# Sliding-window attention: unscaled sums joined by row transfers, and background steps queued behind projections

## The chip, the cores and the metric

The kernel runs on one core of a Trainium2 chip. The metric is the device time of one execution in microseconds (us). Before the change it was 1960.81 us, the median of three runs (1959.38, 1973.70 and 1960.81).

## What is computed

The reference is one inference step of a two-layer decoder with 1024 channels, for a prompt of 1024 tokens and 8 further requests ("samples") with one new token each, 1032 columns in all. Each layer is

```python
h = rms_norm(x);  y = concat(branch(h) * silu(gate(h))) @ w_out;  x = x + rms_norm(y)
```

The even layer has three branches of four heads of 128: a gated delta net (GDN), a dilated sliding-window attention and a cross attention to a memory of 256 rows. The odd layer has a gated linear recurrence (RG-LRU) and the memory attention. Local attention has, for each head, three groups with dilation 1, 4 and 16, each with a query, key and value projection of its own and a window of its own. Each prompt query takes a softmax per group, and the three are merged by their denominators. With m the largest score of a group, l the sum of exp(score - m) and num the sum of exp(score - m) v, a query's result is

```python
M = max(m0, m1, m2);  f_g = exp(m_g - M)
out = sum_g(f_g * num_g) / sum_g(f_g * l_g) * silu(gate)
```

In group 1 the tokens lie ordered by their remainder modulo 4, in group 2 modulo 16, so a query has another place in each group's tiles. The samples' queries attend to caches in HBM (2048 positions at dilation 1, 4, 16, and the memory): "cached attention".

## The kernel before, in words

Channels lie on the 128 partitions, tokens along the free axis. The columns are cut into chunks of 352, 336 and 344. A projection (`proj`, L166) loads 128 output channels of weights (SyncE issues the DMA, 512 KB), splits them in a high and a low part (ScalarE copies, L152; GpSimd or VectorE subtracts, L154), and runs for each chunk 8 x 3 matmuls into one PSUM bank (`mm3`, L162 to L164), so 72 per projection. ScalarE drains the bank (L440, L443). Projections take four rotating banks ("p") in this stage, other work on TensorE takes three ("a") and cached attention one ("c").

The stages are: inputs and norms; `even_gdn` (GDN with its convolutions, chains per head, and the memory heads 0 to 3 between them, to about 650 us); `even_swa` (L902, local attention, about 600 to 1240 us); `out_layer(0)` (L1290); `odd`; `out_layer(1)`. A scheduler of the language orders the instructions on each engine by the kernel's text and priorities, and each engine works through its list in order.

In `even_swa` each of four heads h goes through three groups g. For each there are three projections (q, k, v, tiles `sw`; weights `ws` h g c) and then scores `ss` (TensorE L979), mask and row maximum `P`, `sm` (VectorE L981), and exp with the row sum `sl` (ScalarE L988). Five of the projections of head 0 and its gate are computed earlier, inside `even_gdn` (`swa_ahead`), and reloaded. When the three groups of a head are done, maxima and sums of groups 1 and 2 are brought into the token order of group 0: eight DMAs write them to a DRAM scratch `sd` one element at a time (L995, L999), one reads it back as `al` (L1001). Small VectorE operations of 128x8 and one exp make the scales (`mall`, `sf`, L1005 to L1016), which go out to `fd` (L1017) and come back in group order in four DMAs as `fl` (L1020, L1024). Then the probabilities `P` are scaled in place (VectorE L1055), transposed (`st`, TensorE L1058), copied to SBUF (`spt`, ScalarE L1062) and multiplied by v (`so`, L1064), and the groups are added in `sacc` (VectorE L1072). The result is multiplied by the gate (L917) and written to `mixd`, the DRAM buffer in which the heads of all branches meet. Head 3's gate (weights `wb3`) and, for two other heads, theirs are projected at the end of the stage.

`cached` (L341) does one head of cached attention for the samples: the query row goes to DRAM (`qmd`, `sqd`) and comes back on 16 partitions each (`mqb`, `sqb`), keys and values come from the cache, GpSimd multiplies (L348, L369), VectorE reduces (L349, L370), TensorE joins partitions (`mx`, `po`). Memory heads are named `mc` layer head, local heads `sc` head. Memory heads 0 to 3 and local heads 0 to 2 stand in `even_swa`, local head 3 in `out_layer(0)`.

`out_layer` (L1290) takes the mixed heads as 12 tiles, in the order of the list `order`: it loads each as `mf` (L1284) and splits it into `mah` (L1279, ScalarE) and `mal` (L1280, VectorE), multiplies eight times by a weight tile (`wo` layer m) for the first two chunks, and then eight times for the third chunk from tiles `mbh`, `mbl`, which also hold the samples' columns. The post-norm (`po`) follows chunk by chunk.

Bulk copies of the caches to the outputs (`o_sw1s` to `o_sw3s`, about 1 MB each) are issued by SyncE, one behind each weight load (L151); the prompt's new keys and values (`o_sw1p` to `o_sw3p`) are issued by ScalarE.

## Time and profile before

| | |
|---|---|
| median of three runs | 1960.81 us |
| span of the profiled execution | 1979.3 us |
| TensorE busy | 1788.5 us (90%) |
| VectorE, ScalarE, GpSimd busy | 1086.6, 705.0, 544.1 us |
| share of the chain that ended last | TensorE 65%, VectorE 14%, DMA 13% |

The profiled execution is a run of its own: its span runs from the first to the last instruction of the trace, it is 0.9% longer than the median, and no device time is listed for it apart from the span. Durations and gaps below are from it. "Granted clock" is the TensorE clock as a share of the full 2.4 GHz; its other level is 1.2 GHz, at which matmuls take about twice as long and count as busy. So time is lost both where TensorE is idle and where it is busy at the low clock.

### The profile page before, as it was taken

How to read it: one execution, taken by the hardware profiler on the slowest of the kernel's cores; microseconds unless marked ns; L12 is line 12 of the kernel's file. 1: busy time of each engine (PE TensorE's matmuls, PEld its weight loads, DVE VectorE, ACT ScalarE, POOL GpSimd, SP SyncE). 2: the span in 40 equal slices, each digit the busy share in tenths (PEclk: the TensorE clock that was granted, in tenths of full speed). 3: DMA queues.
4: the chain of work that ended last, by engine and by line, in shares of the span. 5: the costliest groups of instructions: out<-in, count | busy, mean ns of one | idle time of the engine just before them, and what ended most of it. 6: DMA issues, size and time to landing. Idle time of an engine off the chain costs nothing.

```text
span 1979.3 us, 29251 instructions
## 1 busy us (share of the span) xinstructions
PE 1788.5 (90%) x11337; PEld 1727.8 (87%) x11337; DVE 1086.6 (55%) x2391; ACT 705.0 (36%) x1590; POOL 544.1 (27%) x367
## 2 busy tenths in 40 slices
PE   6999998898998977978987987999799999999996
PEld 6899987898998877978987986899699999898996
DVE  7787759436653232224323427648854766747545
ACT  5355533122332322422422323334533434426432
POOL 3422214222111131133133203312643434330201
PEclk9999998998998988998998997999899999999998
DMA  8435464633335664466676454536572533213454
GB/s 282 174 136 205 150 200 168 208 113 134 135 123 183 152 150 118 119 158 149 142 150 151 119 101 124 166 120 226 202 244 101 181 108 117 77 49 119 141 185 141
DMA packets 206411, 297.83 MB, mean 150 GB/s; under 512 B 73312, under 2 KB 168128, under 8 KB 204352
## 3 DMA queue, kind: packets, MB, share of 16 engines
q1 hardware_dynamic: 106640, 208.09, 34.7%
q10 hardware_dynamic: 99632, 87.88, 14.8%
q8 instruction: 89, 1.46, 0.3%
q14 instruction: 50, 0.41, 0.1%
HBM read 246.54 MB, written 137.37 MB: 194 GB/s over the span
## 4 chain that ended last, share of the span: by engine, by line
PE 65%; DVE 14%; DMA 13%; ACT 4%; issue 2%; ACTq 1%; SPq 1%; POOL 0%; DVEq 0%; POOLq 0%
DMA fd<-sf 3%; DMA sd<-sl 2%; DMA al<-sd 2%; PE ss L979 1%; PE so L1064 1%; DVE tm L677 1%; PE ms L316 1%; PE mo L337 1%; DMA fl<-fd 1%; DMA mc00v<-cache_mem 1%; PE gz L800 1%; PE gt L805 1%; DVE P L1055 1%; DMA mf<-mixd 1%; DVE lacc L1216 1%
## 5 line engine op out<-in xcount | busy, mean ns | idle before, releaser
L981 DVE CUSTOM_DVE_ANT_0 P<-ss,cs 128x128 f32<-128x128 f32 (+1 forms) x96 | 33.0, 351 | 83.4 <-PE ss L979 83.0
L1064 PE MATMUL so<-spt,svt 128*128 128x128 f32 x280 | 43.3, 301 | 16.0 <-ACT spt L1062 13.1
L571 DVE SCALAR_TENSOR_TENSOR acc<-pre,vec,acc 128x1024 f32<-128x1024 f32 x36 | 49.3, 1368 | 13.4 <-ACT acc L569 13.2
L1369 POOL TENSOR_TENSOR y<-y,xr 128x352 f32<-128x352 f32 (+2 forms) x24 | 23.0, 960 | 121.6 <-DVE y L1368 104.1
L988 ACT ACTIVATE P<-P,snm 128x128 f32<-128x128 f32 (+1 forms) x96 | 42.4, 443 | 38.6 <-DVE snm L983 37.5
L1064 PEld LDWEIGHTS so<-spt,svt 128*128 128x128 f32 x280 | 40.4, 214 | 17.4 <-ACT spt L1062 17.4
L1055 DVE TENSOR_SCALAR P<-P,fl 128x128 f32<-128x128 f32 (+1 forms) x64 | 21.5, 414 | 56.4 <-DMA fl<-fd 56.4
L1062 ACT COPY spt<-st 128x384 f32<-128x384 f32 (+2 forms) x48 | 22.2, 477 | 82.1 <-PE st L1058 29.0
L1314 DVE TENSOR_TENSOR ya<-ya,ysq 128x352 f32<-128x352 f32 (+2 forms) x42 | 25.6, 610 | 40.0 <-ACT ysq L1313 39.9
L979 PE MATMUL ss<-sw,sw 128*128 128x128 f32 (+1 forms) x192 | 45.1, 323 | 0.6 <-DVE sm L981 0.6
L322 ACT ACTIVATE pm<-ms,nm 128x256 f32<-128x256 f32 x64 | 29.7, 471 | 42.5 <-DVE nm L320 26.5
L1058 PE MATMUL st<-cs,P 128*128 128x128 f32 x140 | 26.1, 303 | 16.3 <-DVE P L1055 16.3
L337 PE MATMUL mo<-mpt,vt 128*128 128x512 f32 x64 | 33.2, 600 | 4.8 <-DVE gnr L120 3.2
L336 DVE COPY mpt<-mt 128x512 f32<-128x512 f32 x32 | 22.0, 688 | 27.0 <-PE mt L334 26.9
L1171 DVE TENSOR_SCALAR lacc<-lpre,vec 128x1024 f32<-128x1024 f32 x8 | 21.4, 2673 | 25.6 <-ACT lpre L1166 25.6
L1058 PEld LDWEIGHTS st<-cs,P 128*128 128x128 f32 x140 | 19.9, 159 | 17.2 <-issue 8.7
L316 PE MATMUL ms<-kt,qm 128*128 128x256 f32 x128 | 33.7, 388 | 0.0
L979 PEld LDWEIGHTS ss<-sw,sw 128*128 128x128 f32 x192 | 32.0, 189 | 1.2 <-DVE sm L981 0.9
L1328 POOL COPY mg<-mixs 128x8 f32<-128x8 f32 x24 | 8.9, 370 | 86.2 <-DVE mbl L1331 12.5
L1174 DVE SCALAR_TENSOR_TENSOR lacc<-lpre,vec,lacc 128x1024 f32<-128x1024 f32 x24 | 32.3, 1346 | 0.2
L677 DVE TENSOR_TENSOR tm<-bl,xi 128x1 f32<-128x1 f32 (+30 forms) x31 | 30.3, 977 | 2.6 <-DMA bl<-aqd 2.1
L318 DVE TENSOR_REDUCE nm<-ms 128x2 f32<-128x512 f32 x32 | 22.0, 686 | 17.6 <-PE ms L316 17.6
(2142 smaller groups left out, 7293.6 us busy)
## 6 DMA issues: line engine op xcount, KB each, us to landing
o_sw3s<-cache_swa SPq DMA_DIRECT2D x64, 1023.5 KB
o_sw2s<-cache_swa SPq DMA_DIRECT2D x16, 1022.0 KB
gaq<-aqd ACTq DMA_DIRECT2D x20, 512.0 KB
mf<-mixd SPq DMA_DIRECT2D x20, 344.0 KB
aqd<-aq ACTq DMA_DIRECT2D x4, 1024.0 KB
o_sw3p<-sw ACTq DMA_DIRECT2D x8, 512.0 KB
mixd<-lgt ACTq DMA_DIRECT2D x8, 512.0 KB
o_sw1s<-cache_swa SPq DMA_DIRECT2D x8, 508.0 KB
```

What stands on the lines that cost most here:

```text
L316: T.matmul(ps[:, b * 256:(b + 1) * 256], q[:, (b0 + b) * P:(b0 + b + 1) * P], kt[:, h, :], start=True, stop=True)
L322: S.activation(pr[:, b2 * 2 + b, :], ps[:, b * 256:(b + 1) * 256], AF.Exp, bias=nm[:, b0 + b:b0 + b + 1], scale=SC, accum_out=lt[:, b0 + b ...
L337: T.matmul(po, vt[:, kb, h, :], st, start=kb == 0, stop=kb == 1)
L571: V.scalar_tensor_tensor(acc, pre[:, j:j + 1024], vc("gconv", ti * 4 + j), acc, ALU.mult, ALU.add)
L677: V.tensor_tensor(t3, bl[:, 0:i, i][:, None, :].broadcast_to([P, i, i]), xi[:, 0:i, 0:i].rearrange("p j c -> p c j"), ALU.mult)
L979: T.matmul(po, q[:, bb * P:(bb + 1) * P], k[:, k0:k0 + w], start=True, stop=True)
L981: V.tensor_tensor_reduce(dst, po, mask, 1.0, NEG, ALU.add, ALU.max, accum_out=m[:, g, bb:bb + 1])
L988: S.activation(dst, dst, AF.Exp, bias=nm[:, g, bb:bb + 1], scale=SC, accum_out=l[:, g, bb:bb + 1])
L1055: V.tensor_scalar(dst, dst, fs, None, op0=ALU.mult)
L1058: T.transpose(tr[:, w:w + P], dst[:, j * P:(j + 1) * P], ident)
L1064: T.matmul(po[:, (bb % 4) * P:(bb % 4 + 1) * P], vtk[g][:, kb, :], pt[:, o:o + P], start=st, stop=sp_)
L1174: V.scalar_tensor_tensor(acc[:, :1024], pre[:, j:j + 1024], vc("lconv", ti * 4 + j), acc[:, :1024], ALU.mult, ALU.add)
```

## The change

The diff below is cut to its core.

- **Background steps.** `start` puts a generator in one of the lanes "cached", "group" and "combine". `tick`, called behind each chunk of a projection (and each chunk of `out_layer`), takes one step from each lane and pins its instructions behind the last instruction issued so far on every engine. `drain_lanes` runs what is left.
- **Groups.** Each group's scores, exp, transposes and products (`group`) run in six such steps, behind the chunks of the projections that follow. The probabilities stay unscaled; the sums `num` (tiles `snum`, three) are copied out of PSUM by ScalarE, in group order.
- **Join.** `combine` transposes maxima and sums of a head into 48 rows (`slt`, `srow`), writes them to `sd` as rows of 512 bytes, reads them as 8 rows by seven DMAs (`al`, token order of each group), makes the scales on 8x128 tiles, writes `fd`, reads each group's 1024 scales back on all partitions (`sfb`, 512 KB each), and multiplies and adds the three `num` on VectorE. The joins of heads 0 to 2 run behind the next head's chunks, that of head 3 is drained at the end of the stage.
- **Moves.** Gates of local heads 1 to 3 and query and gate of memory head 3 are projected in `even_gdn`, kept in DRAM and reloaded. The memory attention of head 3 (`mem_attend`) moves from there to the end of `even_swa`. Cached attention becomes steps of the lane "cached": in `even_swa` memory heads 0 to 2 and local heads 0 to 2, in `out_layer(0)` local head 3 and memory head 3, drained behind the eighth weight tile. `o_sw1p` to `o_sw3p` are issued by SyncE. In `order`, memory head 3 and local head 3 (11 and 7) are last. The cached attention of the odd layer becomes steps too.

```diff
+    def tick():
+        for lane in list(lanes):
...
+            last = {}
+            for i in reversed(nc.cur_bb.bb.instructions):
+                if i.engine in pinned and i.engine not in last:
+                    last[i.engine] = i
...
+            with ExitStack() as after:
+                for ins in last.values():
+                    after.enter_context(tc.issue_after(ins))
+                try:
+                    j[1] = next(j[0]) - 1
...
-                if h < 3:
+                if h < 2:
                     mem_head(h + 1)
                 else:
-                    for key in ((0, 0, 1), (0, 0, 2),):
+                    for key in ((), (), (("q3",), ("g3",), (1,)), ((0, 0, 1), (0, 0, 2), (2,), (3,)))[h]:
                         swa_ahead(me, x, key)
...
+            def combine(h, ml, nums, done):
+                ps = ptile(f"slt{h}")
+                T.transpose(ps[0:48, :P], ml.rearrange("p i g b -> p (i g b)"), ident)
+                rows = sp.tile([48, P], F32, name=f"srow{h}", tag="srow", bufs=1)
+                S.copy(rows, ps[0:48, :P])
...
+                nc.sync.dma_start(out=sd.rearrange("i g b p -> (i g b) p"), in_=rows)
+                yield 1
...
+                nc.sync.dma_start(out=al[:, :, 0, :], in_=sd[:, 0].rearrange("i b p -> b i p"))
...
+                for i in range(2):
+                    for nb in range(2):
+                        nc.sync.dma_start(out=al[nb * 4:nb * 4 + 4, i, 1, :].rearrange("a (r n) -> a r n", r=4),
+                                          in_=s1[nb][:, i])
+                    nc.sync.dma_start(out=al[:, i, 2, :].rearrange("b (q n) -> b q n", q=16), in_=s2[i])
+                yield 2
...
+                S.activation(f, f, AF.Exp, scale=SC)
...
+                nc.sync.dma_start(out=fd.rearrange("g (b p) -> b g p", b=8), in_=f)
+                yield 1
...
+                    fb = sp.tile([P, 1024], F32, name=f"sfb{h}{g}", tag="sfb", bufs=2)
+                    nc.sync.dma_start(out=fb, in_=fd[g][None, :].broadcast_to([P, 1024]))
...
+                V.tensor_tensor(nums[0], nums[0], gt, ALU.mult)
+                done(nums[0])
...
+                    start("group", group(h, g, raw, ml, nums))
+                    if g == 2 and h < 3:
+                        lanes["group"].append([then("combine", combine(h, ml, nums, lambda acc, h=h: put(h, acc))), 0])
                 for f, i in (((mem_cached, 0), (mem_cached, 1)), ((mem_cached, 2), (swa_cached, 0)),
-                             ((mem_cached, 3), (swa_cached, 1)), ())[h]:
-                    f(ca, 0, i)
+                             ((swa_cached, 1), (swa_cached, 2)), ())[h]:
+                    start("cached", f(ca, 0, i))
+            sh0.close()
+            xa = mix_tiles(0, sxa)
...
+            drain_lanes("cached", "group", "combine")
+            mem_attend(sp, 0, 3, qm, gm, gm, tags=("spr", "spt"))
+            mix_put(xa, order[-2], gm)
...
+            start("combine", combine(3, ml, nums, lambda acc: last.update(acc=acc)))
             w0 = out_weights(0, 0, "a")
-            for k in order[:-1]:
+            for k in order[:-2]:
                 mix_load(0, xa, k)
+                tick()
+            drain_lanes("combine")
+            mix_put(xa, order[-1], last["acc"])
...
+            for f in late:
+                start("cached", f(ca))
             for m in range(8):
                 one(m, (0, 1), xs, "a", None if m else w0)
-                if late:
-                    late.pop(0)(ca)
+                if m == 7:
+                    drain_lanes("cached")
...
-    order = [0, 1, 2, 3, 8, 9, 10, 11, 4, 5, 6, 7]
+    order = [0, 1, 2, 3, 8, 9, 10, 4, 5, 6, 11, 7]
...
-    late = [lambda ca: swa_cached(ca, 0, 3)]
+    late = [lambda ca: swa_cached(ca, 0, 3), lambda ca: mem_cached(ca, 0, 3)]
```

Three places show how the instructions are moved (lines of the kernel before in the first list of each pair, of the changed one in the second; the number behind a name tells tiles of one name apart).

The first is VectorE at the join of head 0, which before stands in one piece (`mc01` is cached attention of memory head 1):

```order
L1013 TENSOR_TENSOR mall_6662<-mall_6662 128x8
L1014 TENSOR_TENSOR mall_6662<-mall_6662 128x8
L357 TENSOR_REDUCE mc01mr<-mc01mx 1x8
L1015 RECIPROCAL mall_6662<-mall_6662 128x8
L359 COPY mc01mr<-mc01mr 1x8x16
L1016 SCALAR_TENSOR_TENSOR sf_6663<-sf_6663,mall_6662 128x24
L361 COPY mc01mq<-mc01mr 1x128
L1055 TENSOR_SCALAR P_6145<-P_6145,sf_6663 128x128
```

```order
L996 TENSOR_SCALAR snm_7342<-sml_6903 128x2
L421 TENSOR_REDUCE mc00op<-mc00v_7210 128x128
L1052 TENSOR_TENSOR smm_7390<-al_7284 8x128
L1053 TENSOR_TENSOR smm_7390<-smm_7390,al_7284 8x128
L498 COPY sqkv<-ws110p_7407 128x8
L994 ISA spr_7341,sml_6903<-ss_7434,cs 128x256
L994 ISA sml_6903 128x1
L1054 TENSOR_TENSOR sf_7391<-al_7284,smm_7390 8x128
```

Afterwards the join of head 0 (`al`, `smm`, `sf`) stands among the score steps of head 1 (L994, L996), and no scaling of probabilities follows it.

The second is TensorE at the end of `even_swa`, where the first matmuls of `out_layer(0)` (`wo00p`) follow:

```order
L1058 MATMUL st_10861<-cs,P_9377 128x128 x2
L1064 MATMUL so_10831<-spt_10846,svt_10260 128x128 x2
L355 MATMUL sc2mx<-cs,sc2sm 1x128
L1064 MATMUL so_10851<-spt_10857,svt_10260 128x128 x2
L1064 MATMUL so_10851<-spt_10866,svt_10260 128x128 x2
L362 MATMUL sc2mx<-cs,sc2mq 128x1
L162 MATMUL wo00p_10956<-mah_10704,wo00ah_10874 128x352
L163 MATMUL wo00p_10956<-mal_10705,wo00ah_10874 128x352
```

```order
L352 MATMUL ms_10727<-kt_278,smq_10583 128x256 x2
L370 MATMUL mt_10740<-cs,pm_10719 128x128 x4
L373 MATMUL mo_10739<-mpt_10745,vt_279 128x512
L370 MATMUL mt_10748<-cs,pm_10719 128x128 x4
L373 MATMUL mo_10739<-mpt_10753,vt_279 128x512
L1032 MATMUL slt_10778<-cs,sml_9307 48x128
L162 MATMUL wo00p_10887<-mah_10581,wo00ah_10768 128x352
L162 MATMUL wo00p_10939<-mah_10581,wo00ah_10768 128x336
L162 MATMUL wo01p_11010<-mah_10581,wo01ah_11005 128x352
L162 MATMUL wo01p_11051<-mah_10581,wo01ah_11005 128x336
```

Afterwards ten of the twelve tiles of `wo00` and `wo01` (both chunks, all four "p" banks) stand before `mem_attend`'s last half; behind the transpose `slt` of the join of head 3 come only the 24 matmuls for the last two tiles, 11 and 7.

The third is TensorE in `out_layer(0)`. Before, the last step of memory head 3 stands in the midst of the projections of local head 3; afterwards the whole second half of it stands behind the first matmuls of the third chunk (`wo00p` to `wo02p`, from `mbh`, `mbl`):

```order
L163 MATMUL ws302p_9589<-h0l_115,ws302h_9557 128x336
L373 MATMUL mc03po<-cs,mc03op 128x8
L164 MATMUL ws302p_9589<-h0h_114,ws302l_9558 128x336
L162 MATMUL ws302p_9589<-h0h_116,ws302h_9557 128x336
L163 MATMUL ws302p_9589<-h0l_117,ws302h_9557 128x336
```

```order
L162 MATMUL wo02p_12266<-mbh_11326,wo02bh_12255 128x344
L163 MATMUL wo02p_12266<-mbl_11327,wo02bh_12255 128x344
L164 MATMUL wo02p_12266<-mbh_11326,wo02bl_12256 128x344
L405 MATMUL mc03mx<-cs,mc03sm 1x128
L414 MATMUL mc03my<-cs,mc03mq 128x1
L426 MATMUL mc03po<-cs,mc03op 128x8
L185 MATMUL po00c<-cs,ya_10925 128x1 x3
L426 MATMUL mc03po<-cs,mc03op 128x8
L427 MATMUL mc03po<-cs,mc03sm 128x8
L162 MATMUL wo00p_11937<-mbh_11822,wo00bh_11932 128x344
```

Between the query's transpose `mq03t`, which stands behind the last matmul of `wo07` for the first two chunks, and `mc03mx` there are 72 matmuls.

## Rows read from the trace of the kernel before

**Rows 1.** The page: span, and busy time of TensorE (matmuls).
```profile
span 1979.3 us, 29251 instructions
...
PE 1788.5 (90%) x11337; PEld 1727.8 (87%) x11337; DVE 1086.6 (55%) x2391; ACT 705.0 (36%) x1590; POOL 544.1 (27%) x367
```

**Rows 2.** Stretches: start:end, length, busy PE, PEld, DVE, ACT, POOL, granted clock, DMA share.
```profile
600.00:660.00 60.00, 48.65 (x280) 46.62 (x279) 19.56 (x67) 13.62 (x35) 11.92 (x5) 0.89 0.59 203
720.00:770.00 50.00, 26.84 (x156) 26.17 (x155) 12.39 (x47) 7.75 (x16) 8.53 (x4) 0.76 0.60 138
880.00:920.00 40.00, 22.93 (x129) 22.28 (x128) 10.97 (x42) 5.93 (x13) 5.43 (x3) 0.74 0.62 108
1030.00:1070.00 40.00, 19.01 (x107) 18.35 (x107) 9.62 (x41) 4.55 (x10) 1.35 (x2) 0.74 0.65 113
1170.00:1260.00 90.00, 65.81 (x387) 62.59 (x386) 53.51 (x82) 25.41 (x51) 20.76 (x16) 0.85 0.41 111
```

**Rows 3.** The chain that ended last, 712 to 766 us: start, us, what.
```profile
713.00 0.63 SPq L999
...
714.35 8.32 DMA sd<-sl
722.75 12.39 DMA al<-sd
...
737.39 13.36 DMA fd<-sf
...
751.47 7.36 DMA fl<-fd
...
765.82 0.29 PE ws110p L164
```

**Rows 4.** Waits 560 to 1260 us: who for whom, us in total, times, longest.
```profile
DVE P L1055 <- DMA fl<-fd: 56.4, 4, 15.6
DVE mall L1005 <- DMA al<-sd: 54.6, 4, 16.0
...
ACT ws022h L152 <- DMA o_sw1p<-sw: 25.3, 1, 25.3
...
ACT spt L1062 <- DMA o_sw2s<-sr1r: 13.1, 1, 13.1
```

**Rows 5.** Groups of instructions on the page: busy and mean ns, idle before, releaser.
```profile
L981 DVE CUSTOM_DVE_ANT_0 P<-ss,cs 128x128 f32<-128x128 f32 (+1 forms) x96 | 33.0, 351 | 83.4 <-PE ss L979 83.0
...
L322 ACT ACTIVATE pm<-ms,nm 128x256 f32<-128x256 f32 x64 | 29.7, 471 | 42.5 <-DVE nm L320 26.5
...
L336 DVE COPY mpt<-mt 128x512 f32<-128x512 f32 x32 | 22.0, 688 | 27.0 <-PE mt L334 26.9
```

**Rows 6.** Tiles `mf` and `mqb`: instructions, duration ns min/median/max, first and last start.
```profile
L1280 DVE TENSOR_TENSOR mal<-mf,mah x20: 851/869/2780, 1216.7 to 1821.6; 128x688 fp32r<-128x688 f32 x20
...
L348 POOL TENSOR_TENSOR mc03k<-mc03k,mqb x2: 2386/2396/2406, 1010.7 to 1013.0; 128x1024 f32<-128x1024 f32 x2
```

**Rows 7.** Groups of instructions on VectorE, 560 to 1260 us, shapes apart.
```profile
L370 DVE TENSOR_REDUCE sc2op<-sc2v 128x128 f32<-128x1152 f32 x3 | 6.7, 2218 | 0.0
...
L917 DVE TENSOR_TENSOR sacc<-sacc,sg 128x1024 f32<-128x1024 f32 x3 | 5.1, 1710 | 0.0
...
L370 DVE TENSOR_REDUCE mc03op<-mc03v 128x128 f32<-128x1024 f32 x2 | 4.0, 1992 | 2.4 <-POOL mc03v L369 2.4
```

**Rows 8.** The chain that ended last, single transfers: start, us, what.
```profile
597.76 3.44 DMA mixd<-gz
...
710.40 1.22 DMA qmd<-mq01r
...
998.71 6.82 DMA qmd<-mq03r
1005.54 4.98 DMA mqb<-qmd
```

**Rows 9.** A busy stretch of `out_layer(0)`; columns as in rows 2.
```profile
1250.00:1260.00 10.00, 10.00 (x66) 10.00 (x65) 3.37 (x3) 4.36 (x11) 3.48 (x3) 1.00 0.22 63
```

400 lines of the change are left out of this document (200 added, 200 removed).

## The prediction

> **What bounds the kernel now.** I read the page first. TensorE is busy for 1788.5 of 1979.3 us, 90% [rows 1]; so at best 190 us of idle time and what is lost at the low clock can go, and the question is which stretches hold them and whether the change reaches these. The next view is busy time by stretch. Between 560 and 1260 us, where local attention runs, five stretches are bad [rows 2]: in each the reader is to set TensorE's busy time against the length, and to look at the granted clock, which is a mean of its two levels 1.2 and 2.4 GHz. Idle are 11.4, 23.2, 17.1, 21.0 and 24.2 us, together 96.8. Where matmuls run at the low clock they take twice as long (0.29 us at 765.8 us, behind the wait [rows 3], against 66 matmuls in 10 us, 0.152 each, at full clock [rows 9]), so (1 - clock) x busy time is roughly what a stretch loses besides: 5.4, 6.4, 6.0, 4.9 and 9.9, together 32.6. The five stretches hold 129 us that are no work.
>
> What ends these waits stands in the chain and in the list of waits. From 713 to 759 us the chain is a round trip through DRAM [rows 3]: maxima and sums out, element by element, 8.3 us, back 12.4, scales out 13.4, back 7.4, with VectorE's work between (735.1 to 737.4) taking 2.3 and TensorE idle for want of projections: only five of nine were left to hide it. VectorE waits 56.4 us for `fl` and 54.6 for `al`, four times each [rows 4], one for each head. These are four of the five stretches. The fifth, 600 to 660, is the end of the delta net, where the chain passes the transfer `mixd` of 3.4 us [rows 8], and where ScalarE waits 25.3 us with the next weights behind the transfer `o_sw1p` in its own queue [rows 4].
>
> **The round trip.** The change takes the scales off the probabilities: sums come first, scales are applied to the finished sums, so transposes and products no longer wait for a join. For heads 0 to 2 the join then stands among the next head's nine projections, 9 x 72 x 0.152 = 98 us of TensorE's work [rows 9], and takes about 30 us itself (below), so it is covered three times over. The stretches at 720, 880 and 1030 go whole (61.2 us idle and 17.3 at low clock); what is late next there are single transfers (a residual, below). The transfers of elements become rows: 48 rows out instead of eight DMAs. VectorE's scaling of 96 pieces and 16 additions go, 24 operations of 128x1024 come; VectorE was busy for 24 to 59% of these stretches [rows 2], so I cost that at nothing within the heads; without the projections beside it, it would cost what head 3's join does. Gates projected in the delta net instead of the end are the same work for TensorE elsewhere, and fill it where it waited for `mixd`; `o_sw1p` leaves ScalarE's queue. So the stretch 600 to 660 goes too, but for the residual. Queued behind the moved copies on SyncE are weight loads, which are issued some four projections ahead: covered for 4 x 72 x 0.152 = 44 us.
>
> **The end of local attention** keeps its waits. Behind the last projection nothing is left but `wo00` and `wo01` for the first two chunks, held to the four banks. The list of VectorE there, up to the transpose `slt`: 10 splits at 0.87 (8.7) [rows 6], 3 reductions of cached head 2 at 2.2 (6.7) [rows 7], 12 pieces of 128x512 at 0.69 (8.3), 16 masks and scalings at 0.35 (5.6) [rows 5], 3 low parts taken like splits (2.6): 31.9. To it comes what it waits for: a first load as long as `mixd`, 3.4 [rows 8], four exps of the memory head at 0.47 (1.9) [rows 5], and some 16 of that head's matmuls and transposes at low clock, 0.29 each (4.6) [rows 3]: 42 us. TensorE has 120 matmuls and about 60 small ones there, 27 us at 0.152: idle 15.
>
> Then the join of head 3 stands alone: transpose and copy 0.7; rows out 2; seven issues at 0.63 (4.4) [rows 3] and a landing of 2; VectorE and exp 2.3 as before; scales out 2; two broadcasts of 512 KB 5; six operations of 128x1024 at 1.71 (10.3) [rows 7]; a split 1.6. Sum 30.3, beside 12 matmuls (1.8): idle 28.5. No row shows a small row transfer of this form. The nearest are the query rows `qmd`, 1.22 and 6.82 us [rows 8], and I take 2, nearer to the shorter, since the bulk copies that made others long have mostly run by then; a broadcast lies between 3.4 (512 KB to DRAM) and 10 (two after one another at 4.98) [rows 8].
> The Trainium skill (DMA: Bandwidth & Descriptors, Anatomy of one DMA) gives 2.0 us plus the bytes over 436 GB/s, fitted on GpSimd's path; the join would be 1 to 2 us shorter by it, and the forecast too. The trace does not bear it out under load: `mqb`, 64 KB, took 4.98 us [rows 8], the rule says 2.2.
>
> At the low clock I take what the stretch 1170 to 1260 shows, 15% [rows 2], of 29 us of work: 4.4. The end costs 15 + 28.5 + 4.4 = 48 us in place of 34 before.
> The Trainium skill (TensorE: Matmul & The Clock Gate, HAM oscillation) tells of a kernel in which each tile of k waits for its load and starts cold; `wo00` comes tile by tile here. By it the 27 us would all run at half speed and the forecast be 8 us later, 1917. The old end was fed in the same manner and shows 0.85, not 0.5 [rows 2].
>
> **Memory head 3 in the output stage** is a new wait. Its steps are drained behind the eighth weight tile, and TensorE has 72 matmuls (10.9 us) before it waits for them in order; the post-norm's sums and the last tile's matmuls queue behind. The chain: query transpose and copy 0.4, row out 2, `mqb` 5.0 [rows 8], two multiplications on GpSimd at 2.4 [rows 6] 4.8, a reduction 1.2, maximum and exp like the join's chain 2.3, two multiplications 4.8, a reduction 2.0 [rows 7], closing 1, split 0.9: 24.4. Exposed: 13.5, between 9 (`mqb` as short as a row) and 18 (the row out at 6.82).
>
> **Residual.** Steps are pinned behind chunks, and each that takes a loaded tile can stall an engine with drains behind it. From below this is nothing, from above 38 us, the two waits of ScalarE on its own transfers [rows 4]. Between these I take 16, about what the stretch 600 to 660 lost to transfers of this sort (16.7) [rows 2]. The odd layer's cached heads move beside work that hid them already: nothing, at most 5 either way.
>
> **Sum.** Gone are 129 us, new are 48 + 13.5 + 16 = 77.5: 52 us less. Against the profiled span that is 1927; it is 18.5 us longer than the median, whose runs do the same work, so I take the same 52 off the median: 1909 us.
>
> **Rivals.**
> *More is hidden.* The memory head and the join of head 3 shrink to 36 us, memory head 3 to 9, no residual: 129 - 45 = 84 us, 1877. For it: VectorE has slack in the heads [rows 2]. Against: the order shows both chains alone.
> *The transfers stay slow*, so that the change doesn't do what it says: rows land like elements, 8.3, 12.4 and 13.4 us [rows 3], because the queue is shared with bulk copies. Joins of heads 0 to 2 stay hidden; head 3's grows by 24: 1933. For it: `qmd` of 6.82 us is a row transfer already [rows 8].
> *All upper ends at once.* The join with three landings of 6.8 and slow broadcasts (67 for the end), 18 for memory head 3, 38 of residual: 123 of 129 are given back, 1955, within 1%, which is about what a measurement of this kernel tells from no change.
> *Slower: pinned steps stall at their transfers in the heads.* Three joins and six cached heads stand at fixed places in the engines' lists, each taking tiles from DMAs. If each stalls ScalarE or VectorE as `spt` behind `o_sw2s` did, 13.1 us [rows 4], and TensorE with it, that is 9 x 13.1 = 118 us, with the end and memory head 3 180 against 129: 2011. It decides from (129 - 62) / 9 = 7.5 us of stall on TensorE for each, and is over 1% slower from 9.6. For it: 25.3 and 13.1 [rows 4] are such waits. Against: four banks give 4 x 24 x 0.152 = 14.6 us of slack before a late drain stops TensorE, and steps are spread over several chunks.
> The Trainium skill (TensorE: Matmul & The Clock Gate, Architectural detail) calls ScalarE's and VectorE's queues strict FIFO, which is this rival's mechanism; the trace agrees that weights' casts wait behind a transfer for 25.3 us [rows 4].
>
> **How the numbers follow.** Forecast 0.52, more hidden 0.15, slow transfers 0.10, upper ends 0.12, slower 0.11. Faster by over 1% are the first three, 0.77; within it 0.12; slower 0.11. The range runs from a little under the best case, 1872, to a little over the case of upper ends, 1962, where only the slower rival is outside.
>
> **What would show it.** Right: between 700 and 1150 us no idle stretch of over 5 us on TensorE, and VectorE waiting for `al` about 10 us in one go, at the end alone; an idle TensorE of some 28 us between the transpose `slt` and the last 12 matmuls of `wo00` and `wo01`, with seven DMA issues and six long operations in the chain; a gap of 10 to 18 us before the maximum of memory head 3 in the output stage. Wrong: ScalarE or VectorE waiting on loads in the heads for over 7 us each time with TensorE idle beside it; or the transfers of rows landing at 8 us and more; or a clock near 0.5 all through the end.

## The result and the profile after

The changed kernel took 1942.01 us (median of four runs, 1941.31 to 1943.99), the kernel before 1963.86 beside it (four runs, 1959.38 to 1973.70): a ratio of 0.9874, with a 95% interval of 0.9835 to 0.9912. In a second comparison it took 1936.65 against 1976.41, a ratio of 0.9801 (0.9776 to 0.9826). So it is faster by 22 to 40 us. The forecast was 52: the direction was right, the size too large, by a third against the second comparison and more than double against the first. Each ratio here and below is to runs of the kernel before on the same chip at the same time. "The changed kernel, again" is a second profile of the changed kernel, taken beside the second comparison.

The page of the changed kernel, beside [rows 1]: span, TensorE, and the shares of the chain that ended last.

```profile
span 1942.2 us, 29187 instructions
...
PE 1789.0 (92%) x11341; PEld 1729.4 (89%) x11341; DVE 1081.1 (56%) x2302; ACT 716.3 (37%) x1610; POOL 540.2 (28%) x367
...
PE 73%; DVE 15%; DMA 5%; ACT 3%; issue 2%; ACTq 1%; POOL 1%; SPq 0%; DVEq 0%; POOLq 0%
```

TensorE's work is the same; the DMAs' share of the chain falls from 13 to 5%. Busy time by stretch, columns as in [rows 2]; first of the kernel before, from the first projection of head 1 to the last of head 3:

```profile
693.80:1149.90 456.10, 394.32 (x2535) 388.57 (x2535) 141.71 (x415) 132.43 (x314) 124.57 (x68) 0.93 0.60 139
```

and of the changed kernel the end of the delta net, the same three heads, the end of local attention in two parts (before and behind the transpose `slt`), and the start of the third chunk in the output stage:

```profile
600.00:660.00 60.00, 54.51 (x354) 54.03 (x353) 16.96 (x58) 14.90 (x36) 9.53 (x4) 0.94 0.46 171
717.50:1102.40 384.90, 382.25 (x2539) 377.69 (x2537) 154.32 (x356) 139.51 (x331) 128.78 (x72) 1.00 0.54 182
1102.40:1154.20 51.80, 41.76 (x219) 34.40 (x217) 30.61 (x65) 19.83 (x52) 4.02 (x4) 0.89 0.33 106
1154.20:1184.20 30.00, 7.69 (x26) 6.77 (x25) 17.96 (x23) 4.44 (x10) 0.36 (x2) 0.56 0.25 76
...
1258.80:1295.90 37.10, 23.47 (x102) 20.67 (x101) 14.89 (x34) 5.50 (x12) 8.64 (x5) 0.69 0.52 159
```

The heads are nearly ideal: 2.7 us idle in 384.9, at full clock, where 61.8 were idle before and the clock was 0.93. In the end of the delta net 5.5 us idle are left of 11.4. What else is left stands in the last three lines. The join of head 3, in the changed kernel's chain that ended last:

```profile
1154.90 1.44 DMA sd<-srow
...
1157.36 1.56 DMA al<-sd
...
1164.06 1.35 DMA fd<-sf
1165.43 0.34 SPq L1074
1165.82 5.05 DMA sfb<-fd
1170.89 1.92 DVE snum L1080
1172.84 1.93 DVE snum L1082
1174.76 1.89 DVE snum L1084
1176.68 1.92 DVE snum L1086
1178.62 1.24 DVE snum L1087
```

It is a chain with little beside it: each transfer and each of the five long operations starts where the one before ends, and TensorE works for 7.7 of the 30.0 us. The second exposed chain is memory head 3's cached attention, drained behind the eighth weight tile (1258.8 us):

```profile
1260.05 5.41 DMA qmd<-mq03r
...
1265.53 6.62 DMA mqb<-qmd
...
1274.63 2.38 POOL mc03k L393
1277.01 7.28 issue
...
1284.32 1.91 POOL mc03v L420
...
1286.25 1.94 DVE mc03op L421
```

The query's trip to DRAM and back alone is 12 us. While it runs the DMA engines are full (the share of 1.05 in the first row below); three of the head's four loads of keys and values (1.5 MB) and others are issued at the same moment, which is the likely reason, though no run varied it. A weight load (`wo01bf`) is late there too, and TensorE waits for its split as it waits for the head:

```profile
1259.00:1271.20 12.20, 7.34 (x45) 6.49 (x43) 1.90 (x4) 2.58 (x5) 0.00 (x0) 0.93 1.05 332
...
ACT wo01bh L152 <- DMA wo01bf<-wout: 6.2, 1, 6.2
...
PE mc03po L426 <- DVE mc03op L421: 4.6, 1, 4.6
PE wo01p L162 <- ACT wo01bh L152: 4.4, 2, 4.2
```

The whole third chunk, first before and then after the change:

```profile
1333.80:1394.00 60.20, 57.69 (x357) 56.22 (x355) 50.33 (x129) 30.72 (x62) 12.11 (x12) 0.94 0.59 199
...
1258.80:1337.00 78.20, 64.14 (x366) 60.40 (x364) 50.33 (x120) 29.09 (x61) 16.85 (x14) 0.85 0.64 208
```

Of the 18.0 us that it is longer, 11.6 are idle time of TensorE (14.1 in place of 2.5); by the prediction's formula, (1 - clock) x busy time, 6.2 more go to the low clock (9.6 in place of 3.5).

The next table cuts each profile at the starts of six matmuls: the last of local attention's projections (`ws322`), the last of `wo01` for the first two chunks, the last of `wo07` for them, the last of `wo07` for the third chunk, the first of the odd layer (`wq10`), and the last of its output (`wo17`), behind which every profile has 18 to 19 us more. The points are read from rows such as these two of `wo07` (the two times are the first and the last start):

```profile
L164 PE MATMUL wo07p<-mah,wo07al x24: 313/320/325, 1247.1 to 1258.8; 128*128 128x352 f32 x12, 128*128 128x336 f32 x12
...
L164 PE MATMUL wo07p<-mbh,wo07bl x12: 313/320/402, 1328.5 to 1337.0; 128*128 128x344 f32 x12
```

| us | to last projection | to `wo01` | to `wo07` | third chunk | to odd layer | odd layer and its output | span |
|---|---|---|---|---|---|---|---|
| before | 1149.9 | 107.5 | 76.4 | 60.2 | 47.4 | 519.3 | 1979.3 |
| before, again | 1146.9 | 108.0 | 77.7 | 62.6 | 46.3 | 518.1 | 1978.3 |
| changed | 1102.4 | 81.8 | 74.6 | 78.2 | 54.0 | 532.5 | 1942.2 |
| changed, again | 1101.6 | 80.9 | 73.4 | 78.8 | 52.3 | 527.4 | 1933.1 |
| two steps a chunk | 1109.8 | 82.0 | 85.3 | 59.8 | 44.9 | 528.3 | 1928.8 |
| odd layer in one piece | 1106.6 | 82.0 | 75.7 | 77.5 | 53.6 | 519.7 | 1933.8 |
| both | 1103.8 | 80.9 | 82.5 | 59.3 | 45.5 | 516.3 | 1907.0 |
| join first | 1099.8 | 67.8 | 76.1 | 77.9 | 51.9 | 535.0 | 1927.2 |
| gate 3 at the end | 1093.3 | 86.7 | 72.6 | 75.4 | 58.3 | 529.1 | 1934.1 |
| heads unpinned | 1128.8 | 76.9 | 72.7 | 86.4 | 48.5 | 531.6 | 1963.6 |
| transfers twice | 1115.1 | 82.8 | 71.6 | 80.1 | 53.2 | 529.7 | 1951.3 |
| extra traffic | 1107.6 | 81.3 | 71.8 | 80.4 | 52.0 | 527.6 | 1939.4 |
| memory head 3 in the delta net | 1107.1 | 61.4 | 71.4 | 75.2 | 53.2 | 527.5 | 1914.5 |
| all three edits | 1101.6 | 71.1 | 80.6 | 55.4 | 55.4 | 520.9 | 1903.7 |
| cached memory head 3 beside the join | 1102.2 | 76.2 | 86.3 | 57.3 | 48.1 | 519.7 | 1908.5 |
| late losses undone, memory head 3 in the delta net | 1115.5 | 59.7 | 83.0 | 60.7 | 48.7 | 515.0 | 1901.2 |

In the first two columns together the change gains 73.2 us (1257.4 to 1184.2), more than forecast. It then gives back 18.0 in the third chunk, 6.6 between it and the odd layer, and 13.2 in the odd layer (16.2, 6.0 and 9.3 by the second profile of each kernel). One profile of a stage is not exact: to the last projection the profiles in which nothing ahead of it was edited lie between 1099.8 and 1109.8, and those with the same end of local attention take 80.9 to 82.0 there.

### The profile page after: what moved, and what is told of

It reads as the page before. It is cut to its first block, busy times and chain, and to the rows that moved or that the text cites. A ratio compares the mean times of both kernels' runs of the same rounds, so it can differ in the third digit from the quotient of the medians.

```text
span 1942.2 us, 29187 instructions
## 1 busy us (share of the span) xinstructions
PE 1789.0 (92%) x11341; PEld 1729.4 (89%) x11341; DVE 1081.1 (56%) x2302; ACT 716.3 (37%) x1610; POOL 540.2 (28%) x367
## 4 chain that ended last, share of the span: by engine, by line
PE 73%; DVE 15%; DMA 5%; ACT 3%; issue 2%; ACTq 1%; POOL 1%; SPq 0%; DVEq 0%; POOLq 0%
PE ss L992 1%; PE so L1025 1%; PE mo L373 1%; DVE tm L734 1%; PE ms L352 1%; PE gz L857 1%; PE gt L862 1%; DMA mf<-mixd 1%; PE st L1015 1%; PE mt L370 1%; DVE lacc L1270 1%; DVE got L934 1%; DVE xi L736 1%; DMA o_memv<-vf 1%; PE svp L977 1%
## 5 line engine op out<-in xcount | busy, mean ns | idle before, releaser
L994 DVE CUSTOM_DVE_ANT_0 spr<-ss,cs 128x128 f32<-128x128 f32 (+1 forms) x96 | 31.9, 348 | 84.9 <-PE ss L992 84.5
L1001 ACT ACTIVATE spr<-spr,snm 128x128 f32<-128x128 f32 (+1 forms) x96 | 42.2, 441 | 40.0 <-DVE snm L996 39.8
L628 DVE SCALAR_TENSOR_TENSOR acc<-pre,vec,acc 128x1024 f32<-128x1024 f32 x36 | 49.2, 1366 | 13.4 <-ACT acc L626 13.2
L978 DVE COPY svt<-svp 128x512 f32<-128x512 f32 x24 | 15.5, 684 | 41.6 <-PE svp L977 36.1
L1025 PE MATMUL so<-spt,svt 128*128 128x128 f32 x280 | 38.3, 275 | 0.2 <-ACT spt L1019 0.2
L1228 DVE SCALAR_TENSOR_TENSOR lacc<-lpre,vec,lacc 128x1024 f32<-128x1024 f32 x24 | 37.4, 1560 | 0.2
L1025 PEld LDWEIGHTS so<-spt,svt 128*128 128x128 f32 x280 | 36.3, 191 | 0.5 <-ACT spt L1019 0.5
L1225 DVE TENSOR_SCALAR lacc<-lpre,vec 128x1024 f32<-128x1024 f32 x8 | 19.4, 2419 | 23.7 <-ACT lpre L1220 23.7
L898 DVE TENSOR_TENSOR guu<-guu,gsc 128x128 f32<-128x128 f32 x28 | 8.0, 284 | 38.5 <-PE gsc L897 38.4
L162 PE MATMUL wo00p<-mah,wo00ah 128*128 128x352 f32 (+1 forms) x24 | 8.6, 401 | 22.5 <-ACT mah L1334 22.5
L370 PEld LDWEIGHTS mt<-cs,pm 128*128 128x128 f32 x128 | 17.5, 147 | 13.2 <-issue 8.0
L352 PE MATMUL ms<-kt,qm 128*128 128x256 f32 x112 | 28.7, 387 | 0.0
```

Of the source, the lines that this page charges most:

```text
L352: T.matmul(ps[:, b * 256:(b + 1) * 256], q[:, (b0 + b) * P:(b0 + b + 1) * P], kt[:, h, :], start=True, stop=True)
L370: T.transpose(pt[:, b * P:(b + 1) * P], pr[:, b, kb * P:(kb + 1) * P], ident)
L628: V.scalar_tensor_tensor(acc, pre[:, j:j + 1024], vc("gconv", ti * 4 + j), acc, ALU.mult, ALU.add)
L994: V.tensor_tensor_reduce(pr[:, bb, :w], po, mask, 1.0, NEG, ALU.add, ALU.max, accum_out=ml[:, 0, g, bb:bb + 1])
L1001: S.activation(pr[:, bb, :w], pr[:, bb, :w], AF.Exp, bias=nm[:, bb:bb + 1], scale=SC, accum_out=ml[:, 1, g, bb:bb + 1])
L1025: T.matmul(po[:, (bb % 4) * P:(bb % 4 + 1) * P], vt[:, kb, :], pt[:, o:o + P], start=st, stop=sp_)
```

## Experiments

**The kernel before, again.** No edit.

> The kernel before, unchanged, for a second profile. Theory A (the profiled execution of the prediction was simply 15 to 18 us longer than the median, in the bubbles at the four joins): this profile has a span near 1962 and the five stretches of the prediction together hold some 15 us less idle time and low clock than the 129 us counted there. Rival B (the stretches are the same every time and the extra 15 us lay elsewhere): the five stretches hold 127 to 131 us again, and another stage is shorter.

The span was 1978.3 us, and the five stretches of [rows 2] show idle times and clocks within 3 us and 0.03 of the first profile, each; together they hold 126 us, where the first had 129. The other runs of the kernel before beside it have a median of 1978.6: so the profiled execution of the prediction was no outlier of the kernel. Theory A fails; rival B's first half holds to 1 us, its second (another stage is shorter) was not seen. It took 1959 to 1974 us in the first comparison and 1970 to 1985 in all later ones, on three chips. Where the first runs were faster was not profiled, and stays open.

**The two late losses.** First, two steps behind each chunk of the output stages:

```diff
                     drain(ci, m, ps[:, :n], n)
                     tick()
+                    tick()
```

> The changed kernel with two background steps behind each chunk of the output stages instead of one, so that memory head 3's cached attention is through before the eighth weight tile ends and nothing is drained. Theory A (its drained chain costs 18 us there and, by the late post-norm, some 7 us more between the output stage and the odd layer): 1942 falls by 20 to 25 us, to 1917 to 1922; the first matmul of the odd layer starts about 20 us earlier. Rival B (the gap moves elsewhere, as GpSimd and VectorE are the bound in that stage): 1936 to 1942.

Measured 1923.05 us, 0.9723 (0.9688 to 0.9758) of the kernel before. The third chunk falls from 78.2 to 59.8, as long as before the change, and the way to the odd layer from 54.0 to 44.9: the late post-norm was a consequence of the same drained chain. But the steps crowd the first weight tiles, which take 85.3 us instead of 74.6: TensorE waits there for VectorE's low parts (`wo03al` 5.4 and `wo06al` 2.6 us, where the changed kernel has 3.6 for the first alone), and the clock is 0.92 in place of 0.98. Theory A holds for the two columns (27.5 us), rival B for 10.7 of them, and the time ends 1 us above theory A's range.

Second, the odd layer's cached heads in one piece, not pinned:

```diff
-                    start("cached", mem_cached(ca, 1, n))
+                    for _ in mem_cached(ca, 1, n):
+                        pass
```

> The changed kernel with the odd layer's three cached memory heads emitted at their old place, in one piece and not pinned. Theory A (the pinned one-column matmul of each cached head stands in TensorE's list behind projections while its operand waits in VectorE's list behind the recurrence, 4 to 9 us each time with low clock after it): 1942 falls by 6 to 10 us, to 1932 to 1936, and TensorE no longer waits in the two stretches after the second and third query projection. Rival B (the odd layer is longer because its start is late, from the output stage): 1940 to 1943.

1933.15 us, 0.9772 (0.9739 to 0.9805). The time alone can't be told from the changed kernel's; the stage can: 519.7 instead of 532.5 and 527.4 us, as before the change, with the same late start. The table bears it out: with the heads in pinned steps, eight profiles have 527.4 to 535.0 us in this column, with the heads in one piece five have 515.0 to 520.9, and the two of the kernel before 519.3 and 518.1. Some 7 us of the difference are idle time of TensorE (17.8 in both profiles of the changed kernel, 10.9 here), the rest its busy time. What TensorE waited for there in the changed kernel, by the list of waits:

```profile
PE mc12mx L405 <- DVE mc12sm L402: 5.5, 1, 5.5
PE mc10my L414 <- DVE lacc L1233: 3.6, 1, 3.6
PE mc11my L414 <- DVE lacc L1233: 3.5, 1, 3.5
```

and the chain into one of these, at 1521 us:

```profile
1521.51 2.31 DVE lacc L1271
1523.91 2.18 DVE lacc L1270
1526.14 1.05 DVE pm L364 x4
1527.19 1.14 DVE lgt L1276
1529.09 0.13 DVE mc10mq L411
1529.37 0.55 PE mc10my L414 x2
```

A matmul of one column stands pinned in TensorE's list, its operand `mc10mq` of 0.13 us stands in VectorE's list behind the recurrence's operations of 2 us each, and the projections `wgo2` stand behind the matmul. With the heads in one piece all three waits are gone from the list, and one of 3.1 us (`mc12po`) is back that the kernel before has too (3.2). The granted clock was 0.84 around the wait of `mc11my` (1611 to 1631 us).

This edit takes off the pin and the steps together. The run "heads unpinned" below tells them apart: its edit acts wherever `bulk_on` is set, the odd layer included, so there the steps stand at the same places of the text without a pin. The three waits are gone in it too, but the stage takes 531.6 us, with other waits for VectorE, two of 3.1 us such as this one:

```profile
PE mc10po L426 <- DVE lpre L1217: 3.1, 1, 3.1
```

So, as far as one profile shows, what costs is that the heads are spread over the chunks beside the recurrence, pinned or not, and not the pin by itself.

Third, both edits.

> Both edits: two background steps behind each chunk of the output stages, and the odd layer's cached heads unpinned. If the two causes are apart, the gains add: 26 to 35 us off 1942, 1907 to 1916, which is where the prediction had put the change. If they are one cause (the late start of the odd layer), it is no faster than the better of the two alone.

1910.18 us, 0.9658 (0.9624 to 0.9692). The ratios of the single runs, each over the changed kernel's 0.9801, give 0.9920 and 0.9970, together 0.969; measured is a little better. The causes are apart. That the time lands on the forecast's 1909 is luck: the kernel before took 1979 beside it, so the gain is 68 us and not 52.

**The changed kernel, again.**

> The changed kernel unchanged, beside the kernel before on the chip of these runs, to have the change itself on more than one chip. Theory A (the kernel before spreads by 1% between chips, the changed one gives a like gain on each): ratio 0.983 to 0.989, and the profile's stages as in the first one within 3 us each. Rival B (the change gains more where the kernel before is slow): where before is 1975 to 1980, the changed one is 1942 to 1946, ratio 0.980 to 0.984.

1936.65 us, 0.9801 (0.9776 to 0.9826). All stages but the last are within 2 us of the first profile; that is 5.1 us shorter. The ratio is at rival B's end, outside theory A's range, though the time is lower than either had. The changed kernel takes 1941 to 1944 us in the first comparison and 1935 to 1944 in this one, so most of the difference between 22 and 40 us is that of the kernel before.

**The end of local attention.** The first two steps of the join of head 3 ahead of the memory attention:

```diff
             drain_lanes("cached", "group", "combine")
+            start("combine", combine(3, ml, nums, lambda acc: last.update(acc=acc)))
+            tick()
+            tick()
             mem_attend(sp, 0, 3, qm, gm, gm, tags=("spr", "spt"))
...
-            start("combine", combine(3, ml, nums, lambda acc: last.update(acc=acc)))
```

> The changed kernel with the first two steps of head 3's join (transpose, rows out, rows in) placed ahead of the memory attention of head 3 at the end of local attention. Theory A (the end is a chain: VectorE's list, then the join's transfers, with nothing beside them): the 3 to 5 us of transfers run beside the memory attention, and the stage ends 3 to 6 us earlier; 1942 falls by as much. Rival B (VectorE's list alone sets the end): no change, within 2 us.

1928.39 us, 0.9753 (0.9718 to 0.9787). The end takes 67.8 instead of 80.9 us, 13 less, more than theory A had: not just the transfers lie beside the memory attention, the join and the attention fill each other's waits. In the chain of this run operations of the attention (`nm`, `smg`, `pm`) stand between those of the join, and TensorE's longest wait at the end falls from 20.9 to 11.9 us. The time falls by 8; in the profile the rest of the 13 is lost in the first weight tiles and in the odd layer, which this edit doesn't touch and which varies by as much between profiles.

The memory attention of head 3 back in the delta net (as before the change: `mem_head(3)`, loads of `q3`, `g3` and `mem_attend` taken from the end; the gate of head 1 moves to the last place in the delta net with it):

> The changed kernel with memory attention of head 3 back in the delta net, as before the change. Theory A (at the end VectorE's list is what TensorE waits for, and 11 us of it with its waits are that head): the stretch from the last projection to the transpose of maxima and sums shortens by 9 to 14 us, the delta net gets longer by 2 to 6, in all 4 to 10 us faster, ratio 0.975 to 0.979. Rival B (the loads and splits of the output tiles set the end, the memory head lies beside them): the end shortens by under 4 us and the time is the same or slower, ratio 0.980 to 0.984.

1920.32 us, 0.9723 (0.9679 to 0.9767). The stretches before and behind `slt`, to be set beside the lines of 1102.4 and 1154.2 above:

```profile
1107.10:1134.10 27.00, 21.66 (x124) 19.00 (x124) 19.37 (x40) 13.33 (x33) 3.68 (x2) 0.87 0.54 179
1134.10:1168.50 34.40, 14.77 (x82) 13.82 (x82) 19.29 (x24) 6.64 (x13) 0.73 (x4) 0.73 0.30 92
```

The end is 61.4 instead of 81 us (24.8 less before `slt`, 4.4 more behind it); the delta net grows by 5. Theory A holds in kind, and the memory head was worth 20 us there, not 9 to 14; the time falls by 16, so this move was by itself a loss in the change. In the changed kernel VectorE is busy for 30.6 of the 51.8 us before `slt`, where the sum had 31.9 of 42. Its work was sized rightly, its waits, 21.2 us in place of 9.9, were not; the longest in the list is that of its copies for its transposes:

```profile
DVE mpt L372 <- PE mt L370: 6.0, 3, 3.2
```

Head 3's gate at the end (key `(3,)` taken out of the delta net's list, `swa_gate(3, ...)` put ahead of `sh0.close()`):

> The changed kernel with head 3's gate projected at the end of local attention, as before the change, and no longer in the delta net. Theory A (TensorE is idle at the end and not in the delta net, so 72 matmuls cost 11 us there and nothing at the end): 6 to 11 us faster. Rival B (the tiles of the output stage take the place of the normed input, so loads and splits start only when the gate is done, and the end is as much longer as the delta net is shorter): within 3 us of no change.

1934.06 us, 0.9778 (0.9758 to 0.9799), not to be told from the changed kernel. The way to the last of the projections is shorter by 8 to 9 us and the end longer by 4.9 to 5.8, as rival B has it for the greater part. In the kernel's text the output tiles are made where the normed input is given up (`sh0.close()`), and the trace agrees: here the gate's last matmul starts at 1106.0 us and the first split of an output tile at 1106.7, in the changed kernel the last projection's at 1102.4 and the split at 1103.2:

```profile
L1339 ACT CAST mah<-mf x19: 747/768/781, 1106.7 to 1776.7; 128x688 fp32r<-128x688 f32 x19
...
L1334 ACT CAST mah<-mf x19: 748/767/778, 1103.2 to 1784.4; 128x688 fp32r<-128x688 f32 x19
```

**What keeps the heads clean.** Background steps in local attention not pinned (nor, by the same edit, those in the odd layer):

```diff
-                for ins in last.values():
+                for ins in () if bulk_on[0] else last.values():
                     after.enter_context(tc.issue_after(ins))
```

> The changed kernel with its background steps in local attention emitted at the same places of the text but not pinned behind the last instruction of each engine, so that the scheduler places them. Theory A (the heads run without gaps because sums no longer wait for the join): the heads stay within 5 us, from 700 to 1100 us TensorE is idle for under 8 us, and the time is within 1% of 1942. Rival B (it is the pinning that keeps transfers' waits away from TensorE): gaps of 5 us and more at the joins come back, 20 to 60 us slower.

1961.47 us, 0.9919 (0.9893 to 0.9946): 25 us slower than the changed kernel, 18 of it in the three heads, which take 402.7 us with 14.7 idle, in many small waits of TensorE on masks, exps and copies; 12 us idle more than when pinned, 47 less than before the change.

```profile
726.10:1128.80 402.70, 387.96 (x2535) 379.40 (x2534) 163.41 (x351) 139.01 (x329) 125.33 (x70) 0.99 0.49 167
```

So neither expectation holds whole: the pinning is worth 12 of the 59 us of idle time that went, the rest of the change the other 47. Which part of that rest (unscaled sums, transfers of rows, or steps that stand spread in the text) does it, no run separates.

Then the cover of the joins. Transfers issued twice in heads 0 to 2 (a loop of two around the rows out, six of the seven rows in, and each broadcast):

> The changed kernel with the joins' transfers of heads 0 to 2 issued twice (rows out, four of the seven rows in and two more, and the three broadcasts of 512 KB); head 3's stays single. Theory A (the three joins are covered by the next head's projections, as the prediction has it): no change, ratio 0.978 to 0.983 and no gap of over 3 us on TensorE in the heads. Rival B (they are only just covered): 10 us or more slower for each head that shows, ratio 0.985 and more.

1954.95 us, 0.9884 (0.9847 to 0.9921): the heads take 396.9 us, 12 longer, against theory A. SyncE's list of waits has a row that is new in this kernel:

```profile
SPq L1076 <- DMA sfb<-fd: 21.2, 9, 4.4
```

It waits for the first copy to land before it issues the second to the same tile, so the broadcasts are done later, and VectorE's multiplications wait for them, 23.9 us in all where the changed kernel's second profile has 9.8 (the last row below):

```profile
DVE snum L1080 <- DMA sfb<-fd: 12.6, 2, 10.5
DVE snum L1086 <- DMA sfb<-fd: 9.9, 3, 5.5
...
PE ss L992 <- DVE svt L978: 6.2, 1, 6.2
...
DVE snum L1078 <- DMA sfb<-fd: 6.2, 1, 6.2
```

TensorE's one long wait in these heads (6.2 us, at 811 us) is for a copy `svt` of the next group, which stands in VectorE's list just behind the join of head 0. So the run had added waits, not bytes alone. The bytes alone, a copy of 512 KB that nobody waits for behind each broadcast:

```diff
                     nc.sync.dma_start(out=fb, in_=fd[g][None, :].broadcast_to([P, 1024]))
+                    if h < 3:
+                        x2 = dr.tile([P, 1024], F32, name=f"sfx{h}{g}")
+                        nc.sync.dma_start(out=x2, in_=ahead[h + 1,])
```

> The changed kernel with a copy of 512 KB from DRAM to DRAM that nobody waits for behind each of the three broadcasts of heads 0 to 2: the same bytes more on SyncE's queue as in the run with double transfers (and twice as many in HBM), but no instruction of SyncE that waits for an earlier transfer to land. Theory A (double transfers cost 12 us in the heads because SyncE, in order, waits for the first copy before it issues the second, and weight loads and VectorE's additions stand behind): no change against the changed kernel, within 5 us, ratio 0.978 to 0.983. Rival B (it is the bytes: broadcasts and weights land later): 8 us or more slower, ratio 0.984 to 0.990.

1939.74 us, 0.9810 (0.9784 to 0.9837): no change, and heads of 385.3 us, as in the changed kernel. The joins are covered as to bytes. What cost the 12 us is that the broadcasts come later; the path through VectorE's list is seen at one place, and how much of the 12 us SyncE's waits cost besides, by weight loads behind them, stays open.

**All together.** The two late losses undone and the join first:

> The changed kernel with three edits at once: two background steps behind each chunk of the output stages, the odd layer's cached heads unpinned, and the first steps of head 3's join ahead of the memory attention. If the three losses are apart, ratios multiply: 0.9655 (the first two) less 0.4% (the third): 0.959 to 0.964 of the kernel before. If the third only moves the wait into the output stage, 0.965 to 0.968, no better than the first two.

1901.82 us, 0.9617 (0.9582 to 0.9651): the first case, in its middle, though its interval meets that of the first two edits (0.9624 to 0.9692). The end gains 9.8 us over the profile with these two, and the way to the odd layer gives 9.9 back, for a reason that stays open; the profiles differ by 3.3 us in all. So the third edit's gain on top of the first two is not shown.

The same with memory head 3's cached attention beside the join instead of two steps a chunk (the run keeps one step):

> As the run with all three edits, but memory head 3's cached attention is not crowded into the output stage by two steps a chunk: it starts beside head 3's join, at the end of local attention, where TensorE and GpSimd are idle. Theory A (the crowd of two steps costs the output stage 8 to 10 us beside its first weight tiles, and the end has room for it): 3 to 8 us faster than all three edits, ratio 0.956 to 0.961. Rival B (VectorE's list and in-order waits set the end, so each step there lengthens it): 3 to 10 us slower than all three edits, ratio 0.963 to 0.968.

1915.43 us, 0.9682 (0.9646 to 0.9718), 14 us slower than all three edits. Rival B: the waits of that chain come to stand in TensorE's list at the end.

```profile
PE mc03mx L405 <- DVE mc03sm L402: 9.4, 1, 9.4
PE mc03my L414 <- DVE mc03mq L411: 5.0, 1, 5.0
```

Last, the two late losses undone and the memory attention of head 3 in the delta net:

> The changed kernel with two background steps behind each chunk of the output stages, the odd layer's cached heads unpinned and the memory attention of head 3 back in the delta net. If the gains of the single runs hold side by side (0.9655 for the first two, 0.7 to 0.8% for the third): ratio 0.955 to 0.960, faster than all three edits with the join placed first (0.9617). If the output stage gives back what the end gains: 0.961 to 0.966.

1899.16 us, 0.9593 (0.9570 to 0.9616), the first case: 4.1% faster than the kernel before, and by the ratios 2.1% faster than the change as it was made. It is the fastest of all runs, and can't be told from the run with all three edits.

## Why the prediction was off

**Right.** The round trip is gone from the path: 61.8 us idle in the heads became 2.7, the clock 0.93 became 1.00, and VectorE's wait for `al` fell from 54.6 us [rows 4] to 2.5 in all. What was said to be late next in the heads is hardly there. The end's two parts were forecast at 42 and 30.3 us; they are 51.8 and 30.0. The second agrees in part by luck: rows out and in with their issues took 4.0 us where the sum had 8.4, the small operations and the exp 5.0 where it had 2.3. Idle time and low clock in the two, by the prediction's own formula, are 10.0 + 4.6 and 22.3 + 3.4, together 40 where it had 48. The first part is longer because the memory head's chain is worth 20 us, but TensorE works in it for longer too. The Trainium skill (TensorE: Matmul & The Clock Gate, HAM oscillation) tells of a kernel that waits longer for each tile of k than it computes on it, and starts each one cold. The first part is no such case, and the 8 us more that the prediction worked out by it did not come: TensorE was idle for 10.0 of 51.8 us there and its clock was 0.89. Only the join itself, where TensorE works for 7.7 of 30.0 us, shows 0.56.

**The terms that were off.** By stages, the profile lost 37 us where the sum had 52, and 45 by the second profiles of both kernels:

| | forecast | profile | second profiles |
|---|---|---|---|
| to the end of `wo01` (129 gone, 48 and 16 new) | -65 | -73.2 | -72.4 |
| first weight tiles | 0 | -1.8 | -4.3 |
| memory head 3 in the output stage | +13.5 | +18.0 | +16.2 |
| behind it, up to the odd layer | not priced | +6.6 | +6.0 |
| odd layer | 0, at most 5 | +13.2 | +9.3 |

The step that failed most is "The odd layer's cached heads move beside work that hid them already: nothing, at most 5 either way". The work beside them hides their length, but not their place: spread in steps, their small matmuls wait in TensorE's list for an operand in VectorE's. That is the mechanism of the rival *Slower: pinned steps stall at their transfers in the heads* with another cause, an engine's full list instead of a transfer, without the pin too (531.6 us), and in a stage where the rival had not looked. Emitted in one piece the heads gave 8 to 13 us back.

The second is memory head 3, which reached its upper bound of 18, but not by the bound's own reason alone. The row out took 5.41 and `mqb` 6.62 us, where the sum had 2 and 5.0, and the chain from the query's transpose to its end took 33 us and not 24.4. Yet TensorE's idle time grew by 11.6 us, less than the 13.5: the matmuls beside the chain took longer too. What the term left out is the low clock that comes with the idle time, 6.2 us; the sum had priced it for the end of local attention and not here. The sign that was to show it failed as well: there is no gap right before the maximum `mc03mx`; TensorE waited before it for the late weights of `wo01` and `wo02` (6.6 us in all) and behind it for the head's last steps (7.0). And the sum named the post-norm that queues behind the head without pricing it: 6.6 us, which went with the drained chain in the run with two steps a chunk.

Of the residual, taken as 16, some 12 are left: 2.7 us idle in the heads, and between 600 and 660 us 5.5 idle and 3.3 of low clock, where 5.0 of the idle time are a wait inside the delta net and not for a transfer. ScalarE still waits 19.4 us once, up to 668 us, for `o_sw1p`; 3.3 of the 4.3 us that TensorE is idle beside it belong to that same wait inside the delta net. So stalls as the slower rival had them did not reach TensorE, as its "against" said; no run varied the banks that it gives as a reason.

The -73 agrees with the -65 by offsetting errors too: the move of memory head 3's attention to the end, which was inside the 42 us, cost 16 us when it was tried alone.

**From the profile to the median.** "I take the same 52 off the median" was the third failure. The profiled execution of the kernel before (a run's time is 1.8 us above its span, so some 1981) was like its later runs (medians of 1976 to 1979), and 17 us above the median of those that the time was compared with; the changed kernel takes nearly the same in both comparisons. A gain read from a profile of 1979 can't be taken from a median of 1961 whole: the profiles differ by 37 and 45 us, the medians beside each other by 22 in one comparison and 40 in the other.

## What to carry to other kernels

When small chains are cut into steps and queued behind large work, price each step by the engine's list in which its operand is made: here a step of 0.1 us behind a list of 2 us operations stopped the consumer's whole list. Steps that are left over and drained at the end of a stage stand exposed but for the work that happens to lie beside them, and push what is queued behind them; price the low clock that their gaps bring, and spread them faster, or leave them where there is work. Move work to where the bounding engine is idle only after looking whether the memory that it holds lets the next stage's loads start, and price a chain of short operations by its waits from engine to engine, not by its busy time: the memory head at the end cost 20 us. And a profile and a median of other runs are not one baseline.

## What the runs showed of the hardware

Rows of 512 bytes landed in 1.35 to 1.56 us at the join of head 3. The same maxima, sums and scales, moved one element at a time, took 10.4, 4.4 and 11.9 us at that join in the kernel before:

```profile
1170.33 10.38 DMA sd<-sl
...
1187.32 11.94 DMA fd<-sf
```

(8.3 to 13.4 at the join of head 0 [rows 3]). Beside other transfers rows are slow too: the eight rows of a query took 5.41 us where the DMA share was 1.05. In these rows VectorE's time goes with the length of a row and not with the number of values: straight operations on 8x128 took 0.28 us, the 128x8 ones that they replace 0.16 to 0.17, though both hold 1024 values, and one on 128x1024 took 1.23. With a permuted order of the columns in one operand an operation on 8x128 took 0.35 to 0.41 us, one on 128x1024 1.9:

```profile
L1084 DVE TENSOR_TENSOR snum<-snum,sfb 128x1024 f32<-128x1024 f32 x1 | 2.0, 1969 | 0.0
...
L1078 DVE TENSOR_TENSOR snum<-snum,sfb 128x1024 f32<-128x1024 f32 x1 | 1.2, 1226 | 5.6 <-DMA sfb<-fd 5.6
```

And 4.5 MB more in copies on SyncE's queue cost nothing that could be measured, while broadcasts that landed later, so that VectorE waited 23.9 us for them in place of 9.8, came with heads 12 us longer.
